# Row normalisation on one core: contiguous halves of the rows, and no small transfer ahead of the first load

## The chip, the core and the metric

The kernel runs on one core of a Trainium2 chip. A time is the device time of one execution in microseconds (us); the kernel before took 82.33 us, the median of three runs (82.21 to 82.69). A profile is one execution recorded by the hardware, and its span goes from the first instruction to the last. DVE is VectorE, ACT is ScalarE, POOL is GpSimd, SP is SyncE (SPq its queue of DMA issues).

## The reference

Each of 1024 rows of 4096 float32 numbers is divided by its Euclidean norm.

```python
batch, dim = 1024, 4096
x = np.random.randn(batch, dim).astype(np.float32)
norm = np.sqrt(np.sum(x ** 2, axis=-1, keepdims=True) + 1e-12)
return (x / norm).astype(np.float32)
```

So 16.8 MB are read and 16.8 MB are written, and each number is squared once and scaled once.

## The kernel before

The rows are cut into two tiles. A tile holds 128 partitions with R = 4 rows each (64 KB in a partition, 8.4 MB in all), and both tiles have a buffer of their own, so neither load waits for anything. All loads and stores are issued on SyncE's queue.

```python
    N, D = x.shape                       # 1024, 4096
    R = 4
    n_tiles = N // (P * R)               # 2
    x_t = x.rearrange("(p t r) d -> t p (r d)", t=n_tiles, r=R)
    out_t = out_flat.rearrange("(p t r) d -> t p (r d)", t=n_tiles, r=R)
    # ... pools, eps_t and two scratch tiles for the squares ...

    first = scratch_pool.tile([16, D // 32], F32)
    to_front(nc, nc.sync.dma_start(out=first, in_=x[:16, : D // 32]).ins)

    groups = []
    for i in range(n_tiles):
        g = RowGroups(nc, io, stats, scratch, D, R, eps_t)
        load = nc.sync.dma_start(out=g.flat(), in_=x_t[i])
        to_front(nc, load.ins)
        groups.append(g)

    for i, g in enumerate(groups):
        g.square_dve(R - 1)              # sum of squares of row 3 on VectorE
        g.square_act(0)                  # rows 0, 1, 2 on ScalarE
        g.norm(0)                        # sqrt on ScalarE, reciprocal on VectorE
        g.scale(0)                       # row times 1/norm on VectorE
        g.square_act(1)
        g.norm(1)
        g.norm(R - 1)
        g.scale(1)
        g.scale(R - 1)
        g.square_act(2)
        g.norm(2)
        if i < n_tiles - 1:
            g.scale_by_both(2)           # 7/8 on ScalarE, 1/8 on VectorE
        else:
            g.scale(2)
        store = nc.sync.dma_start(out=out_t[i], in_=g.flat())
```

In the pattern `(p t r)` partition p owns eight consecutive rows: tile 0 takes the first four of them, tile 1 the other four. Between two partitions of one tile lie 128 KB in memory. `to_front` moves a transfer's issue ahead of the barrier with which the program begins, in the order of the calls: the small transfer, the load of tile 0, the load of tile 1. The tile `first` is read by nobody; the small transfer brings 512 bytes of each of the first 16 rows. At the end of the program GpSimd waits for the last store to land.

Of the kernel before, what the change touches and what calls it, by code (L numbers as in the profile page):

```python
# [10 lines left out]
F32 = mybir.dt.float32  # L11
# [71 lines left out]
def to_front(nc, load):  # L83

    def move(program):  # L90
        blocks = program.main_func.blocks
        entry = blocks[0].instructions
        if any(i.name == load.name for i in entry):
            return
        body = next(
            b.instructions
            for b in blocks
            if any(i.name == load.name for i in b.instructions)
        )
        at = next(n for n, i in enumerate(body) if i.name == load.name)  # L100
        assert not body[at].sync_info.on_wait
        before = next(
            n
            for n, i in enumerate(entry)
            if i.engine == mybir.EngineType.SP and isinstance(i, mybir.InstDrain)
        )
        entry.insert(before, body.pop(at))

    nc.at_finalize(move)
# [72 lines left out]
@with_exitstack  # L182
def kernel(
    ctx: ExitStack,
    tc: tile.TileContext,
    x: bass.AP,
    axis: bass.AP,
    eps: bass.AP,
    out: bass.AP,
):  # L190
    nc = tc.nc
    P = nc.NUM_PARTITIONS

    assert isinstance(axis, int) and axis in (-1, len(x.shape) - 1)
    eps = float(eps)

    x = x.flatten_outer_dims()
    out_flat = out.flatten_outer_dims()
    N, D = x.shape
    R = 4  # L200
    assert N % (P * R) == 0
    n_tiles = N // (P * R)
    x_t = x.rearrange("(p t r) d -> t p (r d)", t=n_tiles, r=R)
    out_t = out_flat.rearrange("(p t r) d -> t p (r d)", t=n_tiles, r=R)

    io = ctx.enter_context(tc.tile_pool(name="io", bufs=n_tiles))
    scratch_pool = ctx.enter_context(tc.tile_pool(name="scratch", bufs=1))
    stats = ctx.enter_context(tc.tile_pool(name="stats", bufs=n_tiles))

    eps_t = scratch_pool.tile([P, 1], F32)  # L210
    nc.vector.memset(eps_t, eps)  # L211
    sq_act = scratch_pool.tile([P, D], F32)
    sq_dve = scratch_pool.tile([P, D], F32)
    scratch = {"act": sq_act, "dve": sq_dve}


    first = scratch_pool.tile([16, D // 32], F32)
    to_front(nc, nc.sync.dma_start(out=first, in_=x[:16, : D // 32]).ins)  # L218

    groups = []  # L220
    for i in range(n_tiles):
# [6 lines that stand above are left out]
        g.square_dve(R - 1)  # L228
        g.square_act(0)
        g.norm(0)  # L230
        g.scale(0)
# [8 lines that stand above are left out]
            g.scale_by_both(2)  # L240
# [3 lines that stand above are left out]
    gpsimd_waits_for_last_store(nc, store.ins)  # L244
# [35 lines left out]
```

## Time and profile before

| what | value |
|---|---|
| median of 3 runs (lowest, highest) | 82.33 us (82.21, 82.69) |
| span of the profiled run | 80.4 us |
| HBM read, written | 16.79 MB, 16.78 MB |
| start of tile 0's compute, of tile 1's | 22.24 us, 41.60 us |
| issue of tile 0's store on SyncE's queue | 39.13 us |
| square of a row on ScalarE, on VectorE | 3.6 us, 4.4 us |
| scaling of a row on VectorE | 2.35 us |

Start times count from the beginning of the span. In the profile's lines a group is given as line of the kernel, engine, operation, what it writes and reads. The load of a tile is the line `xt<-in_x_dram`, its store `out_dram<-xt`, the small transfer `first<-in_x_dram`. A row of forty digits divides the span, or the part of it that was asked for, into equal slices, and each digit is the busy share of a slice in tenths. A DMA transfer is cut into packets, which sixteen DMA engines move side by side.

### The profile page before, as it was taken

What the parts mean: (1) busy time and instruction counts of PE and PEld (TensorE: products, weight loads), DVE (VectorE), ACT (ScalarE), POOL (GpSimd) and SP (SyncE); (2) the same over time, 40 slices, a digit from 0 to 9 for tenths busy, and PEclk for the clock granted to TensorE, in tenths of its full rate; (3) what the DMA queues carried; (4) which work ended last, traced back from release to release, by engine and by line L of the source; (5) the groups of instructions that cost most, each with busy time, mean ns of one, the idle gap of its engine ahead of it and who ended that gap; (6) DMA issues with size and microseconds to landing.
All of it is one profiled execution on the core that took longest, in us unless ns stands there. A gap on an engine that the chain in (4) does not pass through costs nothing.

```text
span 80.4 us, 95 instructions
## 1 busy us (share of the span) xinstructions
DVE 26.7 (33%) x21; ACT 29.7 (37%) x23; POOL 0.2 (0%) x4
## 2 busy tenths in 40 slices
DVE  0000000000099599970029995999300000000000
ACT  1500000000099999989429999960000000000000
POOL 0000000000000000000000000000000000000000
DMA  9099993999974999966999966999956999938990
GB/s 526 0 522 522 522 391 130 522 522 522 522 326 196 522 522 522 522 261 261 522 522 522 522 261 261 522 522 522 522 228 294 522 522 522 522 163 359 522 522 0
DMA packets 608, 33.56 MB, mean 418 GB/s; under 512 B 80, under 2 KB 96, under 8 KB 96
## 3 DMA queue, kind: packets, MB, share of 16 engines
q1 hardware_dynamic: 608, 33.56, 97.3%
HBM read 16.79 MB, written 16.78 MB: 418 GB/s over the span
## 4 chain that ended last, share of the span: by engine, by line
DMA 51%; ACT 10%; DVE 9%; SPq 1%; issue 0%
DMA xt<-in_x_dram 51%; ACT sq_act L33 9%; DVE xt L64 9%; ACT rstd L53 1%; SPq L223 1%; SPq L218 0%; DVE rstd L59 0%
## 5 line engine op out<-in xcount | busy, mean ns | idle before, releaser
L33 ACT ACTIVATE sq_act<-xt 128x4096 f32<-128x4096 f32 x6 | 21.6, 3608 | 21.7 <-DMA xt<-in_x_dram 21.7
L42 DVE SCALAR_TENSOR_TENSOR sq_dve<-xt 128x4096 f32<-128x4096 f32 x2 | 8.8, 4424 | 25.7 <-DMA xt<-in_x_dram 25.7
L64 DVE TENSOR_SCALAR xt<-xt,rstd 128x4096 f32<-128x4096 f32 x7 | 16.5, 2353 | 0.2
L72 ACT ACTIVATE xt<-xt,rstd 128x3584 f32<-128x3584 f32 x1 | 3.3, 3282 | 0.2 <-DVE rstd L59 0.2
L53 ACT ACTIVATE rstd<-ssq,eps_t 128x1 f32<-128x1 f32 x8 | 2.1, 289 | 0.1
L59 DVE RECIPROCAL rstd<-rstd 128x1 f32<-128x1 f32 x8 | 1.3, 159 | 2.4 <-ACT rstd L53 2.4
L33 ACT ACT_TABLE_LOAD x1 | 1.3, 1283 | 1.7 <-PEq L261 1.7
L53 ACT ACT_TABLE_LOAD x1 | 1.3, 1283 | 0.0
L33 ACT ACTIVATION_READ_ACCUMULATOR sq_act<-xt 128x1 f32 x6 | 1.1, 187 | 0.0
L211 DVE MEMSET eps_t<- 128x1 f32 x1 | 0.1, 59 | 1.8 <-PEq L261 1.8
L78 DVE TENSOR_SCALAR xt<-xt,rstd 128x512 f32<-128x512 f32 x1 | 0.5, 486 | 0.0
L42 DVE DVE_READ_ACCUMULATOR sq_dve<-xt 128x1 f32 x2 | 0.2, 82 | 0.0
L261 POOL MEMSET const-bfloat16-1.0<- 128x1 bf16 x1 | 0.1, 102 | 0.0
L261 POOL MEMSET const-uint8-127<- 128x1 uint8 x1 | 0.1, 101 | 0.0
L261 POOL MEMSET const-float32-0.0<- 128x1 f32 x1 | 0.1, 99 | 0.2 <-issue 0.2
L261 POOL MEMSET const-float32-1.0<- 128x1 f32 x1 | 0.1, 98 | 0.0
## 6 DMA issues: line engine op xcount, KB each, us to landing
xt<-in_x_dram SPq DMA_DIRECT2D x2, 31.2
out_dram<-xt SPq DMA_DIRECT2D x2, 22.5
first<-in_x_dram SPq DMA_DIRECT2D x1, 8.0 KB, 1.7
```

Of the source, the lines that this page charges most:

```text
L33: self.nc.scalar.activation(out=sq_a, in_=self.x[:, r], func=ACT_F.Square, accum_out=self.ssq[:, r : r + 1],)
L42: self.nc.vector.scalar_tensor_tensor(out=sq_v, in0=self.x[:, r], scalar=1.0, in1=self.x[:, r], op0=ALU.mult, op1=ALU.mult, accum_out=self ...
L53: self.nc.scalar.activation(out=self.rstd[:, r : r + n], in_=self.ssq[:, r : r + n], func=ACT_F.Sqrt, bias=self.eps_t,)
L59: self.nc.vector.reciprocal(out=self.rstd[:, r : r + n], in_=self.rstd[:, r : r + n])
L64: self.nc.vector.tensor_scalar_mul(out=self.x[:, r], in0=self.x[:, r], scalar1=self.rstd[:, r : r + 1])
L72: self.nc.scalar.activation(out=self.x[:, r, :cut], in_=self.x[:, r, :cut], func=ACT_F.Copy, scale=rstd,)
L78: self.nc.vector.tensor_scalar_mul(out=self.x[:, r, cut:], in0=self.x[:, r, cut:], scalar1=rstd)
L211: nc.vector.memset(eps_t, eps)
L223: load = nc.sync.dma_start(out=g.flat(), in_=x_t[i])
L261: nc = _bacc.Bacc("TRN2", target_bir_lowering=False, num_devices=1)
```

## The change

Tile 0 becomes the first 512 rows and tile 1 the last 512 rows: partition p of a tile holds four consecutive rows, and the next partition's rows follow directly in memory, so that a tile is one contiguous piece of 8.4 MB. This makes each transfer a plain contiguous stretch of memory. The small transfer, whose place is ahead of the first load, is taken out together with its tile.

```diff
     R = 4
     assert N % (P * R) == 0
     n_tiles = N // (P * R)
-    x_t = x.rearrange("(p t r) d -> t p (r d)", t=n_tiles, r=R)
-    out_t = out_flat.rearrange("(p t r) d -> t p (r d)", t=n_tiles, r=R)
+    x_t = x.rearrange("(t p r) d -> t p (r d)", p=P, r=R)
+    out_t = out_flat.rearrange("(t p r) d -> t p (r d)", p=P, r=R)
 ...
     sq_act = scratch_pool.tile([P, D], F32)
     sq_dve = scratch_pool.tile([P, D], F32)
     scratch = {"act": sq_act, "dve": sq_dve}
-
-
-    first = scratch_pool.tile([16, D // 32], F32)
-    to_front(nc, nc.sync.dma_start(out=first, in_=x[:16, : D // 32]).ins)
 
     groups = []
```

## The prediction

> **What bounds the kernel now.** I read the page first: busy shares, the forty slices with their DMA rows, the DMA queue.
>
> ```profile
> DVE 26.7 (33%) x21; ACT 29.7 (37%) x23; POOL 0.2 (0%) x4
> ...
> GB/s 526 0 522 522 522 391 130 522 522 522 522 326 196 522 522 522 522 261 261 522 522 522 522 261 261 522 522 522 522 228 294 522 522 522 522 163 359 522 522 0
> DMA packets 608, 33.56 MB, mean 418 GB/s; under 512 B 80, under 2 KB 96, under 8 KB 96
> ...
> q1 hardware_dynamic: 608, 33.56, 97.3%
> ```
>
> No engine is busy for more than 37% of the span, and the one DMA queue fills 97.3% of the sixteen DMA engines. The GB/s row counts a packet in the slice where it starts, so its beat of 522 and 130 is only counting. There are 608 packets: 512 of 64 KB (four transfers of 128 partitions), 16 of 512 B (the small transfer) and 80 of 4 bytes, which are the completion marks, 16 for each of five transfers. Then I asked how full the DMA engines are in four stretches of about one transfer each:
>
> ```profile
> 21.40:40.80 19.40, 12.45 (x10) 16.55 (x12) 0.00 (x0) 1.00 1.01 436
> 40.80:60.10 19.30, 14.22 (x10) 11.87 (x10) 0.00 (x0) 1.00 1.00 431
> 60.10:79.40 19.30, 0.00 (x0) 0.00 (x0) 0.00 (x0) 1.00 1.00 435
> ```
>
> The last two columns are DMA share and GB/s. The second load, the first store and the second store run back to back at share 1.00; no gap is left in which compute is waited for. So the kernel is one line of 32 packets of 64 KB on each DMA engine, and only its beginning and its end can give time back. The chain that ended last seems to say something else:
>
> ```profile
> 0.00 0.39 SPq L218
> 0.39 0.06 issue
> 0.44 0.41 SPq L223
> 0.86 0.04 issue
> 0.90 40.68 DMA xt<-in_x_dram
> 41.58 0.02 issue
> 41.60 3.72 ACT sq_act L33 x2
> ...
> 54.58 2.35 DVE xt L64
> ```
>
> It ends with the last scaling at 56.93 us, because after that the engines run nothing; the store that follows it isn't in it. What it shows well is the beginning: the small transfer's issue takes 0.39 us, and the first load's issue stands at 0.44. Last I asked for the DMA packets of the first 2 us, in slices of 0.05 us:
>
> ```profile
> DMA  0000000000000000000010011010099999009000
> DMA packets 48, 1.06 MB, mean 528 GB/s; under 512 B 16, under 2 KB 32, under 8 KB 32
> xt<-in_x_dram SPq DMA_DIRECT2D x2, 31.2
> first<-in_x_dram SPq DMA_DIRECT2D x1, 8.0 KB, 1.7
> ```
>
> The small packets start from 1.0 us on, the load's from about 1.48 to 1.85; nothing moves in the 1.0 us before. The single packet records of the trace make this exact. Small transfer: issue at 0, first packet at 1.02. First load: issue at 0.44, first packet at 1.48, the last engine's first at 1.85. On an engine each 64 KB packet then follows the one before by 2.416 us (seven steps took 16.91 us on the engine that starts earliest); only the first takes longer, 3.04 to 3.13 us until the second starts. The slowest engine ends its last packet at 79.86, its mark lands at 80.20, and the span ends at 80.38.
>
> [...]16 x 65536 B in 2.416 us is 434 GB/s. [...]0.63 us lie between the end of the small transfer's issue (0.39) and its first packet (1.02), and 0.62 between the end of the load's issue (0.86) and its first packet. [...]
>
> **The change part by part.** *Removed:* one transfer on the sync queue: its issue (0.39 us) with the gap behind it (0.05) and 32 tiny packets, which are 0.03 us of an engine's time and lie in an otherwise empty stretch. All of the 0.44 us of issue is on the path, for the first load can't be issued before it and no packet of the load is waiting for anything else. First-packet time of the load: 0 + 1.04 = 1.04 instead of 1.48. *Changed:* addresses of the four large transfers. Partition p reads rows 8p to 8p+3 and then 8p+4 to 8p+7 before; after, rows 4p to 4p+3 of either half. It stays 64 KB in one piece per partition, 128 partitions, the same bytes, so the same 512 packets: 0 us, if the memory isn't slower on it. *Unmoved:* every instruction of VectorE, ScalarE and GpSimd stands in the same order with the same shapes; only the sync queue is one row shorter. The compute of tile 1 starts when its load lands, so it slides with it.
>
> The sum for the slowest engine, before: 1.48 (first packet) + 0.37 (it starts later than the first engine) + 0.71 (its first packet, 3.13 less 2.416) + 32 x 2.416 = 77.31 + 0.52 (mark and end) = 80.39, against a span of 80.4. After: 1.04 + 0.37 + 0.71 + 77.31 + 0.52 = 79.95. The measured median lies 82.33 - 80.38 = 1.95 us above the span, from which 81.9 us follows; equally 82.33 - 0.44 = 81.89.
>
> **The rivals.** *The small transfer warms something.* It may be there so that a first-use cost of the queue or the DMA engines is over before the first load, which would then pay it. For it: even now the load's first packets take 0.6 to 0.7 us more than the later ones, so starting costs something. Against it: the small transfer, which is the cold one, shows none. From issue to first packet it takes 1.02 us and the load after it 1.04; from a completion mark to its landing in the semaphore it is 0.36 us for the small transfer's first engine, 0.38 for the first load and 0.39 for the second. And the issue before lay on top of the load, not beside it, so a cost up to 0.44 us merely breaks even. If the start cost doubled (another 0.7), the time would be 82.33 - 0.44 + 0.7 = 82.6. For 2% slower (1.65 us) it would have to be 2.1 us, over five times all of the small transfer's life as packets (0.36 us from packet to landing).
>
> *The new addresses are slower in memory.* [...]Every per cent on a packet would be 0.77 us, so 2% slower overall needs packets 2.7% longer, 2.48 us. I can't exclude it from a trace that doesn't have the pattern.
>
> *The new addresses are faster.* [...]If the long first packets were normal ones, 0.7 us more would go: 81.2. Nothing in the trace ties those 0.7 us to the addresses.
>
> *The first store misses its place.* It is issued at 39.13, so its packets could start at 40.17; the first engine ends the second load at 40.78. That is 0.6 us in hand. Loads and compute both shift by 0.44 us, so it stays. If it did miss by some tenths of a microsecond, the DMA engines would stand still for just that long, and the time would be 82.0 to 82.3.
>
> **Range and chances.** 81.9 us is the sum. Below, a somewhat better start and the spread of single runs (82.21 to 82.69 before) give 81.55; above, a start cost that eats the gain and a bit of the spread give 82.5. Two per cent is 1.65 us, nearly four times the 0.44 at stake, so faster by it needs an unknown gain of 1.2 us more, where at most 0.7 are visible: 0.02. Slower by it needs either rival far beyond what shows: 0.03. The rest, 0.95, is within 2%.
>
> **What would show it.** Right: the sync queue's first instruction is a load; its first packets stand near 1.04 us; the first compute starts near 21.8 instead of 22.24 and near 41.2 instead of 41.60; share of the DMA queue rises to some 98% with 592 packets; the span is near 79.9. The warm-up rival would show as first packets still near 1.5 us, or as a first load that lands no earlier than 22.2. The address rival would show as loads or stores over 19.4 us from one to the next. The missed place would show as a slice with a lower share near 40 us. Wrong altogether would be a change in where the profile's span begins against the measured time: then span and median would differ by something other than 1.95.

## The result and the profile after

| | before | after |
|---|---|---|
| median of 6 runs each (lowest, highest) | 82.36 us (82.21, 82.69) | 81.87 us (81.80, 81.94) |
| span of the profiled run | 80.38 us | 80.04 us |
| first packet of the first load | 1.48 us | 1.00 us |
| compute of tile 0, of tile 1 starts | 22.24, 41.60 us | 21.93, 41.26 us |

The ratio is 0.9936 with a 95% interval of 0.9917 to 0.9955: half a microsecond less, within 2%. The prediction said 81.9 us.

The page of the changed kernel has these lines for the forty slices and the DMA queue:

```profile
GB/s 524 0 524 524 524 524 328 197 524 524 524 524 229 295 524 524 524 491 197 360 524 524 524 491 66 491 524 524 524 491 33 524 524 524 524 360 164 524 524 0
DMA packets 576, 33.55 MB, mean 419 GB/s; under 512 B 64, under 2 KB 64, under 8 KB 64
...
q1 hardware_dynamic: 576, 33.55, 97.6%
```

The packets have fallen by 32: the sixteen of 512 bytes and their sixteen marks. The queue fills 97.6% of the DMA engines instead of 97.3%. The chain that ended last, in order of time (start, length, what), says where the gain is:

```profile
0.00 0.38 SPq L219
0.38 0.05 issue
0.43 40.80 DMA xt<-in_x_dram
41.24 0.02 issue
41.26 3.72 ACT sq_act L33 x2
```

One issue of 0.38 us now stands ahead of the long DMA piece where two stood before. L219 is the load itself. The DMA packets of the first 2 us, in slices of 0.05 us:

```profile
DMA  0000000000000000000090999000909090000000
```

In slices this short a packet counts in the slice in which it starts, so the digits mark starts. The load's first packets start from 1.00 us on, where the small packets started before, but the last of the sixteen engines starts its first packet only at 1.64. In the stretches of one transfer each, moved forward by 0.44 us, the last column shows the same rates as before:

```profile
20.96:40.36 19.40, 12.45 (x10) 16.55 (x12) 0.00 (x0) 1.00 1.01 436
40.36:59.66 19.30, 14.22 (x10) 11.87 (x10) 0.00 (x0) 1.00 1.00 435
59.66:78.96 19.30, 0.00 (x0) 0.00 (x0) 0.00 (x0) 1.00 0.99 431
```

So the new addresses change nothing that shows in the steady part. Theory: the whole difference is the small transfer's issue, which no longer delays the first load. Rivals: the contiguous addresses bring some of it; the small transfer had warmed something, and a larger gain hides that.

### The profile page after: what moved, and what is told of

It reads as the page before. It is cut to its first block, busy times and chain, and to the rows that moved or that the text cites. A ratio compares the mean times of both kernels' runs of the same rounds, so it can differ in the third digit from the quotient of the medians.

```text
span 80.0 us, 93 instructions
## 1 busy us (share of the span) xinstructions
DVE 26.7 (33%) x21; ACT 29.7 (37%) x23; POOL 0.2 (0%) x4
## 3 DMA queue, kind: packets, MB, share of 16 engines
q1 hardware_dynamic: 576, 33.55, 97.6%
## 4 chain that ended last, share of the span: by engine, by line
DMA 51%; ACT 10%; DVE 9%; SPq 0%; issue 0%
DMA xt<-in_x_dram 51%; ACT sq_act L33 9%; DVE xt L64 9%; ACT rstd L53 1%; SPq L219 0%; DVE rstd L59 0%
## 5 line engine op out<-in xcount | busy, mean ns | idle before, releaser
L33 ACT ACTIVATE sq_act<-xt 128x4096 f32<-128x4096 f32 x6 | 21.6, 3607 | 21.8 <-DMA xt<-in_x_dram 21.8
```

The source lines that it names most:

```text
L33: self.nc.scalar.activation(out=sq_a, in_=self.x[:, r], func=ACT_F.Square, accum_out=self.ssq[:, r : r + 1],)
```

## The experiments

All ratios are to the kernel before, with 95% intervals.

### The two parts of the change apart

Only the small transfer taken out, the tiles interleaved as before:

```diff
-    first = scratch_pool.tile([16, D // 32], F32)
-    to_front(nc, nc.sync.dma_start(out=first, in_=x[:16, : D // 32]).ins)
```

> The small transfer alone is taken out; the tiles stay interleaved. Theory (the whole difference is the small transfer's 0.44 us of issue ahead of the first load): 81.9 us against 82.36 before, ratio 0.994 to 0.995, first packets of the load at 1.00 to 1.04 us. Rival (the contiguous addresses bring the gain, or some of it): 82.1 to 82.4 us. The same run looks at the uneven start: if the spread of the sixteen engines' first packets is again some 0.6 us, the missing small transfer widens it; if 0.37 us, the addresses do.

Measured: 81.81 us, ratio 0.9943 (0.9929 to 0.9957). That is the whole gain of the change. Its load's first packets start from 1.01 to 1.64 us, as in the changed kernel, so the wider spread of the start is not made by the addresses.

Only the new addresses, the small transfer put back into the changed kernel:

```diff
+    first = scratch_pool.tile([16, D // 32], F32)
+    to_front(nc, nc.sync.dma_start(out=first, in_=x[:16, : D // 32]).ins)
```

> Contiguous halves alone, with the small transfer still ahead of the first load. Theory (only the issue counts): 82.35 us, ratio 1.000 within 0.2%. Rival (the addresses bring the gain): 81.9 us, ratio 0.994. Second rival (contiguous addresses cost a little, covered by a larger gain from the small transfer): 82.5 us or more.

Measured: 82.37 us, ratio 1.0012 (0.9998 to 1.0026). The contiguous halves give nothing and cost nothing that can be told from zero. First packets start from 1.48 to 1.89 us.

### Does the small transfer give anything back?

```diff
+    for n in range(3):
+        first = scratch_pool.tile([16, D // 32], F32, name=f"first{n}")
+        to_front(nc, nc.sync.dma_start(out=first, in_=x[:16, : D // 32]).ins)
```

> Contiguous halves with three small transfers ahead of the first load. Theory (each costs its issue of 0.44 us and gives nothing back): 81.87 + 3 x 0.44 = 83.2 us, first packets of the load at about 2.3 us. Rival (the first one warms something and so pays for part of itself): the step from none to one is clearly smaller than half of the step from one to three; for instance 0.25 us for the first, 0.88 for the other two, 83.0 us in all.

Measured: 83.36 us, ratio 1.0126 (1.0109 to 1.0143). The steps are 82.37 - 81.87 = 0.50 us for the first small transfer and 83.36 - 82.37 = 0.99 us for two more, 0.50 each: the first is no cheaper than the others, so nothing shows that it pays back. How sharp is that? The kernel without a small transfer was timed on another occasion (the kernel before had a median of 82.36 us then, and of 82.29 with the other two), and single figures scatter: by the means of the runs the steps are 0.54 us and 0.48 each, by the spans of one execution of each kernel (80.04, 80.41, 81.53 us) 0.38 and 0.56 each. A saving of about a tenth of a microsecond can't be excluded; one of the size of the issue can. The chain of this kernel begins with them:

```profile
0.00 0.39 SPq L218
0.39 0.06 issue
0.44 0.41 SPq L218
0.85 0.04 issue
0.90 0.42 SPq L218
1.32 0.04 issue
1.36 0.42 SPq L223
1.78 0.04 issue
1.82 40.90 DMA xt<-in_x_dram
```

L218 are the small transfers, L223 the load of tile 0. In the packet records the load's first packet starts at 2.41 us. The three issues with their gaps are 0.44, 0.46 and 0.46 us, 1.36 in all; the last of the engines' second packets starts at 6.09 instead of 4.65, 1.44 later; the time grew by 1.49. So a little more than the issue is lost with each, about 0.04 us, for which I have no cause.

The same transfer behind both loads instead of ahead of them:

```diff
         groups.append(g)
 
+    first = scratch_pool.tile([16, D // 32], F32)
+    to_front(nc, nc.sync.dma_start(out=first, in_=x[:16, : D // 32]).ins)
```

> Contiguous halves with one small transfer issued behind both loads instead of ahead of them. Theory (it costs only where it delays the first load's issue): 81.9 us, as without it, with 0.03 us of packets on each engine between the second load and the first store. Rival (one more transfer with its completion costs some time wherever it stands): 82.1 to 82.35 us.

Measured: 81.92 us, ratio 0.9956 (0.9941 to 0.9971), the same as without it. The DMA issues of this kernel, in order of time (start, time from there to the end of the last of the x issues):

```profile
0.00 0.85 SPq L219 DMA_DIRECT2D xt<-in_x_dram  x2
0.90 0.43 SPq L224 DMA_DIRECT2D first<-in_x_dram  x1
38.78 18.17 SPq L242 DMA_DIRECT2D out_dram<-xt  x2
```

The issue costs the queue 0.43 us as before, but at 0.90 us both loads have been issued, and no packet waits for this issue. It is the place that costs, not the transfer.

### Do addresses matter at all?

In two more kernels each partition takes four separate rows, so that a packet is 16 KB (2112 packets in all instead of 576). First, inside the contiguous tiles, rows p, p + 128, p + 256, p + 384 of the tile; the tile is loaded and stored with its rows as a dimension:

```diff
-    x_t = x.rearrange("(t p r) d -> t p (r d)", p=P, r=R)
-    out_t = out_flat.rearrange("(t p r) d -> t p (r d)", p=P, r=R)
+    x_t = x.rearrange("(t r p) d -> t p r d", p=P, r=R)
+    out_t = out_flat.rearrange("(t r p) d -> t p r d", p=P, r=R)
```

> Contiguous tiles without the small transfer, but inside a tile partition p takes rows p, p + 128, p + 256, p + 384, so that each partition's 64 KB are four packets of 16 KB, 16 KB apart between partitions. Theory ([...]addresses and packet sizes of this order cost next to nothing):[...] 82.0 to 82.6 us. Rival (the order of addresses matters to the memory): packets of 16 KB clearly over 0.62 us, 83.5 us or more.

Second, with `"(p r t) d -> t p r d"` in both places: the tiles alternate row by row, and 128 KB lie between partitions.

> The tiles alternate row by row: partition p takes rows 8p, 8p + 2, 8p + 4, 8p + 6 or those between, four packets of 16 KB, 128 KB between partitions. Theory: the same as the kernel with rows p, p + 128 and so on, within 0.3 us (82.0 to 82.6 us), since both have the same packets and differ only in addresses. Rival (addresses matter): the two differ by over 0.5 us.

Measured: 82.28 us, ratio 0.9995 (0.9985 to 1.0005), and 82.67 us, ratio 1.0041 (1.0027 to 1.0055). The first is in the expected range; the two differ by 0.4 us, between what theory and rival expected. The stretches of one transfer each in the second kernel do not show a slow memory:

```profile
21.50:40.80 19.30, 12.45 (x10) 16.55 (x12) 0.00 (x0) 1.00 1.02 435
40.80:60.10 19.30, 14.23 (x10) 11.87 (x10) 0.00 (x0) 1.00 1.01 432
60.10:79.40 19.30, 0.00 (x0) 0.00 (x0) 0.00 (x0) 1.00 1.00 427
```

From the first load's last marks on, the three other transfers take 58.4 us in either kernel by the packet records (79.83 - 21.42 and 80.27 - 21.84). In the changed kernel it is 57.97 (79.52 - 21.55); the 0.44 us are 6 ns for each of the 72 more packets on an engine. The difference is at the beginning; the chain of the second kernel:

```profile
0.00 0.68 SPq L219
0.68 0.04 issue
0.72 41.18 DMA xt<-in_x_dram
```

Its first issue takes 0.68 us, that of the first kernel 0.43 and that of the changed kernel 0.38, and its first packet starts at 1.45 us instead of 1.10 and 1.00. Between the two kernels, then, 0.25 us of the 0.35 are issue, and the other 0.10 lie between the issue's end and the first packet. Here a longer issue of the first load is time on the path, like an issue ahead of it. That the pattern is the reason for the longer issue is argued from these three kernels, not tested further, and it isn't the only thing that sets it: the plain load of tile 1, issued second, takes 0.43 us in the changed kernel and 0.56 us in the next kernel.

### What is left at the start

The kernels from here on try to shorten the start. The first load in two parts of 64 partitions, from two queues at once:

```diff
+            load = nc.sync.dma_start(out=g.flat()[:64], in_=x_t[i][:64])
+            to_front(nc, load.ins)
+            load = nc.scalar.dma_start(out=g.flat()[64:], in_=x_t[i][64:])
+            to_front(nc, load.ins, mybir.EngineType.Activation)
```

> The changed kernel with the first load in two parts of 64 partitions, one issued on SyncE's queue, the other at the same time on ScalarE's. Theory (the start is issue, delay to the first packet and one start cost of each DMA engine, which are the same from either queue): 81.8 to 82.0 us. Rival (the late first packets, 0.64 us from the first to the last engine, come from the one queue's working through 128 partitions): the spread of first packets halves and 0.2 to 0.3 us go, 81.6 us.

Measured: 102.42 us, ratio 1.2438 (1.2412 to 1.2464). Theory and rival both fall. The DMA packets of the first 24 us, in slices of 0.6 us:

```profile
DMA  0099000005990000059900000099000000995000
...
q1 hardware_dynamic: 48, 3.15, 61.1%
q10 hardware_dynamic: 32, 2.10, 40.9%
```

The starts come in bursts every 4.9 us: by the packet records sixteen packets of SyncE's queue (q1), then sixteen of ScalarE's (q10), in turns, eight bursts in all. Each packet takes 4.90 us instead of 2.42 and moves at half the rate. In each burst all sixteen engines write to the same half of the partitions, and the trace has 209 GB/s from 1.5 to 20 us. A second run tells this from two queues as such: the parts are now rows, each of all 128 partitions.

```diff
+            half = R * D // 2
+            load = nc.sync.dma_start(out=g.flat()[:, :half], in_=x_t[i][:, :half])
+            to_front(nc, load.ins)
+            load = nc.scalar.dma_start(out=g.flat()[:, half:], in_=x_t[i][:, half:])
+            to_front(nc, load.ins, mybir.EngineType.Activation)
```

> The first load in two parts by rows, each of all 128 partitions, rows 0 and 1 from SyncE's queue and rows 2 and 3 from ScalarE's at the same time. Theory (in the run that took 102 us it was the halves of the partitions that made each packet 4.9 us: all sixteen engines wrote to the same 64 partitions at a time): packets of 32 KB take 1.21 us again, load 1 lands near 21.9 us, 81.9 us in all. Rival (two queues at once halve the rate): the first load lands near 41 us, 100 us or more. Third possibility: the store is issued earlier or ScalarE starts later by some tenths of a microsecond, without effect on the end.

Measured: 82.06 us, ratio 0.9969 (0.9960 to 0.9978); the first load's parts land at 21.95 and 22.12 us. The stretch from 1.5 to 20 us (DMA share and GB/s stand last), first with halves of the partitions, then with halves of the rows:

```profile
1.50:20.00 18.50, 0.06 (x1) 0.00 (x0) 0.00 (x0) 1.00 0.98 209
1.50:20.00 18.50, 0.00 (x0) 1.04 (x1) 0.00 (x0) 1.00 0.96 413
```

Two queues at once do not halve the rate (413 GB/s); with the halves of the partitions it is halved (209 GB/s). What halves it was not shown; the two halves one behind the other on a single queue were not run. Nothing is gained by the second queue either (the kernel is 0.2 us slower than the changed one): the sixteen first packets start from 1.01 to 1.91 us, no closer together.

The first load as two transfers of two rows each, one behind the other on SyncE's queue:

```diff
-        load = nc.sync.dma_start(out=g.flat(), in_=x_t[i])
-        to_front(nc, load.ins)
+        cuts = (0, 2, R) if i == 0 else (0, R)
+        for lo, hi in zip(cuts, cuts[1:]):
+            at = slice(lo * D, hi * D)
+            load = nc.sync.dma_start(out=g.flat()[:, at], in_=x_t[i][:, at])
+            to_front(nc, load.ins)
```

> The changed kernel with tile 0's load as two transfers of two rows each, both on SyncE's queue, packets of 32 KB. Theory (the start cost is paid once per engine whatever the first packet's size; the second issue lies beside the first part's transfer): 81.85 to 82.0 us, a first packet of 1.21 + 0.6 to 0.7 us. Rival (the start cost grows with the size of the first packets): half of the 0.65 us goes, 81.55 us. What an earlier start of the compute would bring is nothing, as the DMA engines are the limit.

Measured: 83.20 us, ratio 1.0100 (1.0083 to 1.0118), at least 1.2 us worse than either expectation. The start is as the theory had it: an engine's first packet of 32 KB takes on average 0.54 us more than its later ones (0.66 with 64 KB), not half as much, and tile 0 is complete at 21.46 us by its last mark, against 21.55. The loss lies elsewhere: the last packet of the second load takes 3.6 to 4.0 us on all sixteen engines. What had changed there is that compute began with the first half of the tile, so the first store was issued at 31.9 us instead of 38.8.

### A store that is queued too early

To move the store alone, the load is whole again, and part of tile 0's work is left out: rows 1 and 2 of each partition are stored unscaled (first kernel), or only row 2 (second kernel).

```diff
-        g.square_act(1)
-        g.norm(1)
+        if i > 0:
+            g.square_act(1)
+            g.norm(1)
 ... likewise scale(1), and square_act(2), norm(2) and the scaling of row 2
```

> The changed kernel with the work on rows 1 and 2 of each partition of tile 0 left out (they are stored unscaled), so that the first store is issued at about 32 us instead of 38.8; loads as in the changed kernel. Theory (a store that waits in the queue behind the second load for long makes that load's last packets slow, as in the run with the first load in two, where they took 3.7 us instead of 2.42): about 83.2 us, the last packet of the second load again 3.6 to 4.0 us. Rival (the cutting of the first load itself does it): 81.85 us, no packet over 2.5 us after the start.

> The same with only row 2 of tile 0 left out, first store issued at about 34.8 us. Theory of the early store, if the stall has one size once the store is queued before the last packet of the load starts (at 37.9 us): 83.2 us. If it grows with the time in the queue: between 81.9 and 83.2 us, near 82.6. Rival (cutting the load does it): 81.85 us.

Measured: 83.12 us, ratio 1.0120 (1.0087 to 1.0153), with the store issued at 32.26 us, and 83.10 us, ratio 1.0102 (1.0088 to 1.0116), with the store at 34.80. Less work, and 1.2 us more time than the changed kernel. The issues of the two stores, first of the changed kernel, then of the one with the store at 32 us:

```profile
38.82 18.13 SPq L239 DMA_DIRECT2D out_dram<-xt  x2
```

```profile
32.26 25.80 SPq L239 DMA_DIRECT2D out_dram<-xt  x2
```

The DMA packets from 36 to 44 us in slices of 0.2 us, in the same order:

```profile
DMA  7000000009997000000009997000000009997000
```

```profile
DMA  0000000009999000000000000009999000000009
```

In both, the second load's last packets start at about 37.9 us. In the changed kernel the store's follow 2.4 us later; here it is about 3.6 us, and from then on the beat is 2.4 us again. The reverse test keeps the first load in two but lets the compute take the rows of the second part first:

```diff
-        g.square_act(0)
-        g.norm(0)
-        g.scale(0)
+        g.square_act(2)
+        g.norm(2)
+        g.scale(2)
 ... and row 0 in the place of row 2 at the end
```

> The first load in two transfers as before, but the compute takes the rows of the second part first, so that it starts when both have landed and the first store is issued at about 38.8 us. Theory of the early store: no stall, 81.8 to 81.9 us. Rival (cutting the load does it): 83.2 us.

Measured: 81.82 us, ratio 0.9937 (0.9924 to 0.9950), store issued at 38.95 us. The issues of the stores, and the beat from 36 to 44 us, which is whole:

```profile
38.95 18.15 SPq L242 DMA_DIRECT2D out_dram<-xt  x2
```

```profile
DMA  7000000009997000000007999700000007999900
```

So cutting the load is harmless. In the three kernels whose first store was issued 3 to 6 us before the load's last packets start, the time is 1.2 to 1.4 us above that of the changed kernel, and about the same for 3 us as for 6. That the engines have nothing to compute in the meantime isn't enough: in the changed kernel they have nothing to do from 57 us on either, and no packet there takes over 2.45 us. Where between 34.8 and 38.8 us the cost begins, and what makes it, stays open. A load queued behind a load shows no such thing before and after the change: tile 0's last packets take 2.42 us with tile 1's load issued at 0.9 and 0.4 us. A store behind a store was hardly tested: with packets of 64 KB the second store is issued only 0.5 to 1.3 us before the first one's last packets start. In the two kernels with packets of 16 KB it is 2.5 to 3.0 us, and those packets keep their 0.61 us; so do the last packets of the second load there (0.61 to 0.62 us), though the first store is issued 1.1 to 1.6 us before them.

No kernel here beats the changed one by a difference that its interval shows.

## Why the prediction was right

**The bound.** Read as one line of 32 packets on each engine that runs back to back. By the packet records, from the slowest engine's second packet (4.976 before, 4.648 after) to its last mark (79.857, 79.522) it is 74.88 us before and 74.87 after, so no wait for compute shows in it.

**The part removed.** Its 0.44 us were named as wholly on the path. The run without it alone gives the whole gain, the one with it behind the loads gives the same, and three of them cost three times as much. By the medians the size is 0.49 us (82.36 - 81.87) rather than 0.44; by the spans of the profiled executions it is 0.34.

**The sum.** First packet 1.00 us for 1.04. The two terms behind it were misread. The prediction set the earliest second packet against the earliest first one and the latest against the latest, and got 3.04 to 3.13 us; but these belong to different engines. Followed engine by engine (the next packet of an engine is the one that starts as the last one ends), the first packet took 2.92 to 3.33 us before. The slowest engine (the one that ends last) started 0.20 us after the first and took 3.29: 1.48 + 0.20 + 3.29 = 4.98 us, to which 1.48 + 0.37 + 3.13 comes too, so the sum was right in total and wrong in its parts. In the changed kernel the slowest engine again starts 0.20 us after the first, and its first packet takes 3.44 us; the engine that starts last, 0.64 us after the first, has a first packet of only 2.77. So the slowest engine's second packet comes at 1.00 + 0.20 + 3.44 = 4.65 us (from unrounded figures) where the sum has 1.04 + 0.37 + 3.13 = 4.54: the length of the slowest first packet is the term that was mis-sized. The end took 0.52 us as predicted. So the span is 80.04 for 79.95. That the median still met 81.9 is partly luck in a second term: I set the median against the span of one run and took 1.95 us for what lies outside the span. The profiled runs themselves took 82.21 and 81.87 us, 1.83 us above their spans in both. The span came 0.09 us longer than the sum and the rest 0.12 us shorter, which nearly cancels. This is also why span and median differ by something other than 1.95 us, which the prediction had named as a sign of being wrong altogether: with one and the same execution on both sides, the difference has not moved.

**The warm-up rival** was weighed on the right lines: the small transfer's own delays were as short as the later ones. The count of three refutes it for anything near the size of the issue. Something small could speak for it: with one small transfer first packets were spread over 0.37 and 0.41 us, without one over 0.63 us in the changed kernel, whose latest second packet came 0.11 us later than the shift of 0.44 us says. But in the interleaved kernel without it that was only 0.02 us, and with three small transfers the spread was 1.0 us. These are single executions, and either figure is far less than the issue.

**The address rivals.** Slower and faster both fall for the contiguous halves: the ratio is 1.0012 (0.9998 to 1.0026). From the second transfer on, 16, 64 or 128 KB from one partition to the next, packets of 64 KB or 16 KB, the four address patterns all ran at 427 to 436 GB/s. What sets that rate, and whether another order could exceed it, was not shown.

**The missed place.** The store kept its place, as said. But the rival was seen from one side only: being late was weighed, being early was not. A store issued 3 to 6 us before the load's last packets start is what costs, 1.2 to 1.4 us.

**What would show it.** Compute starts came at 21.93 and 41.26 us for 21.8 and 41.2, the share of the DMA queue at 97.6% for some 98%. The count of 592 packets was a slip: the small transfer's sixteen marks go as well, 608 - 32 = 576.

## What to carry to other kernels

In the kernels before and after the DMA engines were full from the first packet to the last (97.3% and 97.6% of the span). What stood ahead of the first load's issue was paid in full (0.44 us of issue, 0.49 us by the medians), and the same small transfer behind the loads cost nothing that can be told from zero (81.92 us against 81.87). In a kernel of this kind, try the order in which the first large load is issued first, and look at how long that issue takes (0.38 to 0.68 us here). Where transfers already moved at some 430 GB/s, another order of addresses won nothing (427 to 436 GB/s in four orders). And issuing a store as early as possible isn't always best (1.2 to 1.4 us were lost here): compare the last load packet's length with and without the store in the queue.

## What the runs showed that I had not expected

- A store queued behind a load before that load's last packet started (issued at 31.9, 32.3 and 34.8 us; last packets from 37.9 us) made those packets 3.2 to 4.0 us long instead of 2.42, on all sixteen engines, and the kernel 1.2 to 1.4 us slower. With the store issued at 38.8 to 39.1 us, those packets took 2.42 to 2.43 us. With packets of 16 KB, a first store issued 1.1 to 1.6 us before the load's last packets lengthened none of them.
- Two loads of 64 partitions each at the same time from two queues moved at half the rate: packets of 4.90 us, 102.42 us in all. Two loads of all partitions from two queues did not (413 GB/s, 82.06 us).
- The issue of one load took 0.38 us with 64 KB in one piece per partition, 0.43 us and 0.68 us with four rows per partition in two patterns. What sets it was not tested.
- The sixteen engines' first packets start 0.37 and 0.41 us apart with one small transfer ahead of the load, 0.50 to 1.0 us apart with none, 1.0 us with three, and before and after the change an engine's first packet takes 2.7 to 3.4 us where the later ones take 2.42; what sets either is open.
